# A two-layer hybrid decoder step: the order of every engine's instructions planned with the timeline model in place of the plain one

## The chip, the cores and the metric

The kernel runs on one core of one Trainium2 chip, in one launch. The metric is the device time of that launch in microseconds; smaller is better. Three timed runs of the kernel before gave 1852.14, 1854.70 and 1857.76 us (median 1854.7).

The core has five engines with an instruction stream each: TensorE (PE in the profile, with its weight loads apart as PEld), VectorE (DVE), ScalarE (ACT), GpSimd (POOL) and SyncE (SP, which here issues nearly all DMAs). Each engine runs its own stream in order, and an instruction that waits for another engine or for a DMA holds up what stands behind it on its engine. So the order of each stream is part of the program.

## The reference, cut to what matters

Two groups of tokens share all weights: a prompt of 256 tokens that starts from zero state, and 8 sequences of 4 new tokens that bring their states along. That is 288 columns, which are carried through together. Two layers follow one another:

```
x = x + 0.5 * swiglu(rmsnorm(x), w_ffn1_gu, w_ffn1_down)          # 1024 -> 2 x 2816 -> 1024
u = rmsnorm(x);  q,k,v,g,a,z,xbc,dt,gate_a,gate_b = split(u @ w_in)
log_a  = log_sigmoid(a @ w_gla_a2 + b) / 16
o_gla  = rmsnorm(gla_chunked(q, k, v, log_a, state_gla)) * silu(g)  # gated linear attention, 4 heads
xs,B,C = split(silu(causal_conv(xbc, state_conv)))
y      = ssd_chunked(xs, softplus(dt + dt_bias), -exp(a_log), B, C, state_ssm) + d_skip * xs
y      = rmsnorm(y * silu(z))                                       # state space part, 32 heads
m      = sigmoid(gate_a) * (o_gla @ w_proj_gla) + sigmoid(gate_b) * (y @ w_proj_ssm)
x = x + m @ w_out
x = x + 0.5 * swiglu(rmsnorm(x), w_ffn2_gu, w_ffn2_down)
...
return rmsnorm(x), new_gla, new_ssm, new_conv                       # states of both groups
```

All inputs and outputs are float32.

## The kernel before, in words

**Big products.** The activations lie transposed, 128 channels by 288 tokens. A float32 product is made of three products in a reduced type (float32r): `weights` (L171) loads a block of 1024 x 128 weights (512 KB) by SP into `wr` (4 buffers), `split` makes its high part `wh` on ScalarE (L158) and the rest `wl = wr - wh` on VectorE (L164; 3 buffers each), and `mm3` runs 24 matmuls of 128 x 128 by 128 x 288 on it: eight pairs `wh` x high and low activations (L177, L178) and eight `wl` x high (L180), all into one PSUM tile `psg` (3 buffers, in places 7).

**Stages of a layer.** `ffn` is 44 such blocks for gate and up, then 24 for the way down; VectorE and ScalarE have a few instructions of 288 columns beside each. `mixer` has `gla` first (the projections q, k, v, then the attention in small matmuls of full float32 into `pst` tiles, 4 buffers) and then `ssd`, which goes through 16 pairs of heads, j = 0 to 15. For each j there is a chain over the engines: `stage_x` (conv: ACT L851, DVE L852, L853, ACT L856, three times DVE L858, ACT L860, DVE L862), `stage_m` (transposes on PE L142, `m` on ACT L1010 to L1014, `xg` on DVE L1018, `xd` on POOL L1021) and `stage_y` (PE L1044 to L1051, DVE L1053, POOL L1059, ACT L1061, DVE L1063; state update PE L1069, DVE L1071). `stage_bc` and `stage_group` (PE L926 to L928, DVE L923) come once for 4 of the j.

**Fillers.** `gla` and `ssd` are generators. At each `yield n` the loop `run` traces n steps of `fillers`, which are the big products that depend on neither: z (16 blocks), g (8), then gate and projection of the GLA branch, then the last gate. So in the traced program small chains alternate with blocks of `mm3`.

**What sets the order.** The program is traced once, in the order of the Python code, inside `tile.TileContext(nc)`. When the context closes, a list scheduler plays the traced program on a model of the machine. When an engine of the model is free, it takes of that engine's instructions those whose inputs are there (in the model) and whose buffers are free, and of those the one traced first. What it takes is the engine's instruction stream; buffers and semaphores follow from it. On the chip the stream is fixed: an instruction that the model thought ready, and that is not, is waited for. In the program as built, 604 of TensorE's 13,077 matmuls stand ahead of one that was traced earlier, 964 of VectorE's 2,202 instructions, and 270 of SP's 809 DMAs. There are no priorities or due times written by hand besides the order of the code.

The lines that the change touches are the opening of the context in `kernel`:

## Time and profile before

| | |
|---|---|
| median of three runs | 1854.7 us |
| the profiled execution | 1855.64 us, of it 1853.4 us span from the first to the last instruction |
| TensorE busy | 1816.3 us (98%), 13,712 matmuls |
| weight loads of TensorE (PEld) | 1750.2 us (94%) |
| VectorE / ScalarE / GpSimd busy | 1292.0 (70%) / 1035.5 (56%) / 237.1 us (13%) |
| mean granted TensorE clock | 0.993 |
| moved by DMA | 325 MB, 176 GB/s in the mean |

Busy time is the time in which at least one instruction of the engine runs. Matmuls are pipelined: a block of equal matmuls shows some 300 ns for each record, while they start 133 ns apart. The idle time before an instruction is put down to the one that ended last of those it waited for. The granted clock is 1.00 where TensorE runs at its full 2.4 GHz; a lower mean says for what share of a stretch it was at 1.2 GHz.

### The profile page before, as it was taken

The numbers are of one execution on the slowest core, as the hardware profiler recorded it, in microseconds if no ns is written. First come the engines' busy times: TensorE is split into PE (matmuls) and PEld (weight loads), VectorE is DVE, ScalarE is ACT, GpSimd is POOL, SyncE is SP. The second block draws the span as 40 slices with busy tenths as digits, with TensorE's granted clock in tenths as the row PEclk, the third lists the DMA queues.
The fourth block names the chain that finished last, engine by engine and source line by source line (L and its number), as shares of the span: only waits on it lengthen the run. The fifth ranks groups of instructions, "written<-read, shape, count | busy, mean of one in ns | idle before, by whom it ended". The sixth has DMA issues, their size and how long they took to land. (4 is left out here: it accounts for less than half of the span.)

```text
span 1853.4 us, 34776 instructions
## 1 busy us (share of the span) xinstructions
PE 1816.3 (98%) x13712; PEld 1750.2 (94%) x13712; DVE 1292.0 (70%) x2202; ACT 1035.5 (56%) x1818; POOL 237.1 (13%) x305
## 2 busy tenths in 40 slices
PE   8999999999999999999999999999999999999998
PEld 8999999888899899999999999998889998999997
DVE  6555577689989767555565556776999887665554
ACT  6444466566767646444454445665776675454443
POOL 1000000024435300000000000000444443000000
PEclk9999999999999999999999999999999999999999
DMA  7555654866777655555555556568667775655553
GB/s 210 165 168 158 167 140 128 265 184 177 211 213 208 179 167 170 170 166 164 166 168 163 165 158 166 136 184 246 166 186 219 199 217 156 176 160 169 160 161 93
DMA packets 613111, 325.41 MB, mean 176 GB/s; under 512 B 17090, under 2 KB 607986, under 8 KB 612948
## 3 DMA queue, kind: packets, MB, share of 16 engines
q1 hardware_dynamic: 612900, 323.07, 61.7%
q8 instruction: 107, 1.75, 0.4%
q14 instruction: 56, 0.46, 0.1%
q10 hardware_dynamic: 48, 0.13, 0.0%
HBM read 292.93 MB, written 30.22 MB: 174 GB/s over the span
## 5 line engine op out<-in xcount | busy, mean ns | idle before, releaser
L158 ACT ACTIVATE wh<-wr 128x1024 fp32r<-128x1024 f32 (+1 forms) x498 | 518.0, 1041 | 470.6 <-PE psg L178 384.9
L177 PE MATMUL psg<-xh,wh 128*128 128x288 f32 x2704 | 744.0, 301 | 3.0 <-DVE cbuf L853 2.3
L178 PE MATMUL psg<-xl,wh 128*128 128x288 f32 x2704 | 738.1, 299 | 0.1
L164 DVE TENSOR_TENSOR wl<-wr,wh 128x1024 fp32r<-128x1024 f32 (+1 forms) x496 | 602.8, 1215 | 147.9 <-ACT wh L158 147.1
L177 PEld LDWEIGHTS psg<-xh,wh 128*128 128x128 f32 x2704 | 511.4, 190 | 9.9 <-issue 6.3
L178 PEld LDWEIGHTS psg<-xl,wh 128*128 128x128 f32 x2704 | 511.5, 189 | 3.5 <-issue 0.9
L180 PE MATMUL psg<-xh,wl 128*128 128x288 f32 x2704 | 416.2, 296 | 0.0
L180 PEld LDWEIGHTS psg<-xh,wl 128*128 128x128 f32 x2704 | 378.6, 189 | 1.1 <-issue 0.9
L177 PE MATMUL psg<-hh,wh 128*128 128x288 f32 x704 | 189.7, 296 | 0.0
L178 PE MATMUL psg<-hl,wh 128*128 128x288 f32 x704 | 189.4, 295 | 0.0
L304 DVE TENSOR_TENSOR t<-t,psg 128x288 f32<-128x288 f32 x88 | 40.0, 454 | 135.2 <-ACT wh L158 123.1
L178 PEld LDWEIGHTS psg<-hl,wh 128*128 128x128 f32 x704 | 132.8, 189 | 0.0
L177 PEld LDWEIGHTS psg<-hh,wh 128*128 128x128 f32 x704 | 132.4, 188 | 0.1
L180 PE MATMUL psg<-hh,wl 128*128 128x288 f32 x704 | 109.2, 296 | 0.0
L301 DVE TENSOR_TENSOR t<-psg,rr 128x288 f32<-128x288 f32 x88 | 40.2, 457 | 90.4 <-PE psg L180 90.4
L180 PEld LDWEIGHTS psg<-hh,wl 128*128 128x128 f32 x704 | 98.9, 188 | 0.0
L858 DVE SCALAR_TENSOR_TENSOR cacc<-cbuf,cw,cacc 128x312 f32<-128x312 f32 x144 | 86.6, 601 | 9.5 <-ACT cacc L856 8.9
L1037 POOL TENSOR_TENSOR st<-st,decs 128x512 f32<-128x512 f32 x64 | 83.5, 1323 | 25.5 <-PE pst L142 24.2
L371 POOL MEMSET cbuf<- 128x3 f32 x4 | 0.3, 108 | 654.6 <-DVE t L324 654.6
L177 PE MATMUL psg<-yh,wh 128*128 128x288 f32 x256 | 70.0, 300 | 0.0
L178 PE MATMUL psg<-yb,wh 128*128 128x288 f32 x256 | 69.2, 297 | 0.8 <-DVE yb L1063 0.8
L177 PE MATMUL psg<-oh,wh 128*128 128x288 f32 x256 | 69.7, 300 | 0.0
(312 smaller groups left out, 2322.9 us busy)
## 6 DMA issues: line engine op xcount, KB each, us to landing
wr<-in_w_ffn_gu_dram SPq DMA_DIRECT2D x176, 512.0 KB
wr<-in_w_in_dram SPq DMA_DIRECT2D x160, 512.0 KB
wr<-in_w_ffn_down_dram SPq DMA_DIRECT2D x64, 448.0 KB
wr<-in_w_ffn_down_dram SPq DMA_DIRECT2D x32, 512.0 KB
st<-in_state_ssm_dram SPq DMA_DIRECT2D x64, 256.0 KB
out_dram<-st SPq DMA_DIRECT2D x64, 256.0 KB
wr<-in_w_proj_ssm_dram SPq DMA_DIRECT2D x32, 512.0 KB
gst<-in_state_gla_dram SPq DMA_DIRECT2D x32, 256.0 KB
```

The source lines that it names most:

```text
L158: A.activation(out=h, in_=raw, func=AF.Copy)
L164: V.tensor_tensor(out=lo, in0=raw, in1=h, op=ALU.subtract)
L177: T.matmul(out, lhsT=h[:, k], rhs=xh[k], start=start and k == 0, stop=False)
L178: T.matmul(out, lhsT=h[:, k], rhs=xl[k], start=False, stop=False)
L180: T.matmul(out, lhsT=lo[:, k], rhs=xh[k], start=False, stop=stop and k == n - 1)
L301: V.tensor_tensor(out=t, in0=pg, in1=r, op=ALU.mult)
L304: V.tensor_tensor(out=h, in0=t, in1=pu, op=ALU.mult)
L371: G.memset(cbufs[i][:, 0:3], 0.0)
L858: V.scalar_tensor_tensor(out=acc, in0=buf[:, i:i + NCV], scalar=w[i], in1=acc, op0=ALU.mult, op1=ALU.add)
L1037: G.tensor_tensor(out=sts[hf], in0=sts[hf], in1=bcast(decs[:, 8 * j + hf:8 * j + 8:2], 2, 128), op=ALU.mult)
```

## The change

`TileContext` gets one more argument. The scheduler then plays the same traced program on another model of the machine, one that follows each instruction through the parts it occupies (the engine's queue, its start, the tail of its write, the clock and the passes of the TensorE array, the DMA queues); the plain model is coarser. Nothing else is edited: the same instructions are traced, with the same shapes, operands and buffers, and the same number of DMAs. What may differ is the order in each of the five streams, and with it which of a tag's buffers a tile gets, where a semaphore is waited for, and where ScalarE has to change its function tables.

```diff
@@ -1246,7 +1246,7 @@
     for i, shape in enumerate(_OUTS):
         args.append(nc.dram_tensor(f"out_{i}_dram", shape, F32, kind="ExternalOutput").ap())
-    with tile.TileContext(nc) as tc:
+    with tile.TileContext(nc, schedule_with_timeline_sim=True) as tc:
         tile_hybrid_step(tc, *args)
     r = run_bass_kernel_spmd(nc, [arrays], core_ids=[0])
```

## Rows read from the trace of the kernel before

**Rows 1.** The page, part 1: busy time, share and instructions of each engine.
```profile
span 1853.4 us, 34776 instructions
PE 1816.3 (98%) x13712; PEld 1750.2 (94%) x13712; DVE 1292.0 (70%) x2202; ACT 1035.5 (56%) x1818; POOL 237.1 (13%) x305
```

**Rows 2.** Windows by stage: first FFN, mixer, two FFNs, mixer, last FFN.
```profile
0.00:236.26 236.26, 230.98 (x1683) 227.10 (x1684) 136.79 (x198) 116.19 (x164) 7.46 (x15) 1.00 0.61 172
236.26:697.86 461.60, 449.55 (x3431) 419.69 (x3430) 378.04 (x718) 294.17 (x598) 113.84 (x143) 0.99 0.68 188
697.86:1149.96 452.10, 451.98 (x3402) 450.57 (x3401) 263.74 (x372) 217.84 (x297) 1.05 (x5) 1.00 0.57 165
1149.96:1608.58 458.62, 448.02 (x3431) 417.97 (x3430) 376.85 (x719) 293.61 (x598) 114.62 (x141) 0.99 0.68 189
1608.58:1853.40 244.82, 235.76 (x1773) 234.85 (x1771) 136.59 (x199) 113.68 (x165) 0.11 (x1) 0.99 0.51 149
```

**Rows 3.** Windows of 50 us: length, busy PE PEld DVE ACT POOL, clock, DMA.
```profile
100.00:150.00 50.00, 50.00 (x376) 50.00 (x375) 27.51 (x39) 23.23 (x32) 0.00 (x0) 1.00 0.55 159
250.00:300.00 50.00, 48.53 (x348) 46.09 (x348) 36.22 (x83) 29.95 (x59) 0.00 (x0) 0.97 0.46 123
350.00:400.00 50.00, 47.49 (x337) 42.33 (x336) 33.36 (x62) 29.97 (x59) 5.84 (x13) 0.97 0.73 207
400.00:450.00 50.00, 46.06 (x349) 42.72 (x348) 49.03 (x94) 32.48 (x70) 22.19 (x27) 0.93 0.60 165
1300.00:1350.00 50.00, 44.56 (x329) 41.52 (x330) 46.87 (x97) 36.66 (x84) 21.47 (x30) 0.95 0.54 148
1350.00:1400.00 50.00, 47.88 (x370) 44.65 (x369) 48.33 (x87) 33.09 (x71) 20.43 (x26) 0.98 0.78 215
```

**Rows 4.** Waits of PE, whole run: total us, times, longest.
```profile
PE psg L142 <- DMA xi<-in_x_prompt_dram: 4.7, 1, 4.7
```

**Rows 5.** Waits of PE in the first mixer (236 to 698 us).
```profile
PE pst L1044 <- DVE xg L1018: 2.3, 2, 1.8
PE pst L142 <- DVE t L138: 0.8, 1, 0.8
```

**Rows 6.** Waits of PE in the second mixer (1150 to 1608.6 us).
```profile
PE pst L142 <- DVE b L138: 1.5, 1, 1.5
```

**Rows 7.** Timeline of PE, 429 to 438 us: start, length, idle before.
```profile
429.97 0.31 PE L928 MATMUL pst<-bcf,b 128*128 128x32 f32 x2
432.07 0.66 PE L1044 MATMUL pst<-m,xg 128*64 128x256 f32 x4 [1.79 <-DVE xg L1018]
...
435.21 0.80 PE L1069 MATMUL pst<-bm,xpk 128*128 128x512 f32 x1 [1.39 <-ACT sh L967]
...
437.37 0.44 PE L177 MATMUL psg<-xh,wh 128*128 128x288 f32 x1
437.61 0.44 PE L178 MATMUL psg<-xl,wh 128*128 128x288 f32 x1
```

**Rows 8.** Timeline of ACT in the same stretch, the last split ahead of it.
```profile
428.83 1.04 ACT L158 ACTIVATE wh<-wr 128x1024 fp32r<-128x1024 f32 x1
```

**Rows 9.** Timeline of DVE, 263 to 265 us.
```profile
263.59 1.20 DVE L164 TENSOR_TENSOR wl<-wr,wh 128x1024 fp32r<-128x1024 f32 x1
264.72 0.21 DVE L138 COPY t<-t 128x128 f32<-128x128 f32 x1
```

**Rows 10.** Groups of PE and DVE by line: count, busy us, mean ns, idle before.
```profile
L1069 PE MATMUL pst<-bm,xpk 128*128 128x512 f32 x64 | 25.3, 461 | 4.6 <-ACT sh L967 2.8 <-DVE bpk L923 1.7
L1018 DVE TENSOR_TENSOR xg<-pst,dtt 128x384 f32<-128x384 f32 x32 | 17.5, 547 | 0.0
```

**Rows 11.** Groups of ACT by line: one of the lines with table loads.
```profile
L607 ACT ACT_TABLE_LOAD x6 | 7.7, 1283 | 0.1
```

**Rows 12.** Waits of SP's queue: total us, times, longest.
```profile
SPq L171 <- DVE wl L164: 740.3, 268, 12.7
SPq L1073 <- DVE st L1071: 38.8, 42, 2.2
```

## The prediction, made before the result was known

> **What bounds the kernel now.** I read the page's busy shares first, then windows by stage, then windows of 50 us, and last the waits and timelines where a window showed a hole. The shares say TensorE: 1816.3 us busy of a span of 1853.4 [rows 1]; 1853.4 - 1816.3 = 37.1 us is all that it idles. The windows by stage put a place to it [rows 2]: 236.26 - 230.98 = 5.3 us in the first FFN, 461.60 - 449.55 = 12.05 us in the first mixer, 0.1 us in the 452 us of the two FFNs between, 458.62 - 448.02 = 10.6 us in the second mixer, and 244.82 - 235.76 = 9.1 us in the last FFN. The first of these is nearly all one wait of 4.7 us for the first input [rows 4], and the last lies behind the last block: output and its transfer. Neither depends on which ready instruction an engine takes first. In the FFN a window of 50 us holds 376 matmuls without a hole, 133 ns each, with VectorE at 27.5 and ScalarE at 23.2 of 50 [rows 3]: no order can speed that up, and there is slack enough that few would slow it.
>
> So the change can act in the mixers, 920 us. There it can gain the idle 12.05 + 10.6 = 22.65 us, and with it what the clock costs: five windows show a granted mean under 1 [rows 3], short by 0.03, 0.03, 0.07, 0.05 and 0.02 of 50 us, together 10.0 us of full-speed work. Where the clock fell, TensorE had just been waiting: after holes of 1.79 and 1.39 us the matmuls start 0.24 us apart, 437.37 to 437.61 [rows 7], which is the 1.2 GHz level, against 0.133 before. I cost a clock loss that goes away with its holes at the whole 10.0 at most. The ceiling of a gain is then 22.65 + 10.0 = 32.65 us.
>
> **The change part by part.** It removes and adds no instruction; it permutes five streams. I take them in turn.
>
> *TensorE's stream.* What can go is a wait of its head while something behind it is ready. The trace shows that such work was there. At 430.28 (429.97 + 0.31) TensorE stops for 1.79 us before L1044, whose `xg` was late on VectorE; later for 1.39 us before L1069; and the first block behind them, at 437.37, needs a `wh` [rows 7]. The last split that ScalarE made ahead of it ended at 428.83 + 1.04 = 429.87 us [rows 8], before the hole began. So 16 matmuls on that `wh`, 16 x 0.133 = 2.1 us, could have stood in front of L1044 and filled its hole; the plain model evidently thought `xg` ready sooner than it was. Both mixers lose most of their idle in holes of this kind [rows 5, 6]: 1 to 2 us for a VectorE or ScalarE result of the chain, with a block behind. Bounds: a model that gets the durations right recovers between nothing (it moves the holes) and all 22.65 us. I take half, 11.3: rows 7 show one hole that a block covers and, 3 us on, a second for which only the rest of that block would be left.
>
> *What the new order brings of its own.* The two mixers are the same code on the same shapes, planned in different circumstances, and they wait at different places: the largest wait of the first is 1.8 us for `xg` [rows 5], of the second 1.5 us for the packed `b` [rows 6]. They take 461.60 and 458.62 us [rows 2]. So 3.0 us per mixer is what an order of this kind is worth by chance, and I charge the new one 2 x 3.0 = 6.0 us of new waits. The clock follows the holes: half of 10.0, so 5.0 comes back.
>
> *VectorE's stream.* At 400 to 450 us it is busy 49.03 of 50 us [rows 3]; its 378 us of work in a mixer of 461.6 [rows 2] don't bound the whole, but there its order decides what TensorE gets. A split `wl` (L164) of 1.20 us was put ahead of the copy L138 of 0.21 us at 263.59 [rows 9], and TensorE waited 0.8 us for the copy [rows 5]. An order could undo such picks or make more of them; this price is in the rival below, and in the forecast inside the two terms above.
>
> *ScalarE's stream.* It is 56% busy [rows 1], so its moves are hidden under TensorE except in the chains. One thing could be added: a function table load costs 1.283 us [rows 11], and another order of `Exp` and `Ln` in the decay chain could add or save some. L607 has 6 of them; 6 more would be 7.7 us on ScalarE and, since it idles 167 of 461.6 us of a mixer [rows 2], I cost them at nothing; uncovered, at 7.7.
>
> *SP's and GpSimd's.* SP's queue waits for its buffers, not the other way round: the weight loads L171 wait 740 us for `wl` to free a raw tile [rows 12]. A state store L1073 put ahead of a load holds it up by at most 2.2 us [rows 12]; a load runs up to four blocks of 24 x 0.133 = 3.2 us ahead, which hides it. Without that cover each of the 42 such waits would cost up to 2.2 us, and that I leave to the range. GpSimd is 13% busy [rows 1]: nothing, unless its one multiply in the chain is picked late, for which the same cover serves.
>
> **The sum.** The profiled execution took 1855.64 us, 2.2 more than its span. 1855.6 - 11.3 + 6.0 - 5.0 = 1845.3. That execution lies 0.9 us over the median of the runs, so a median of 1844 to 1846; I say 1845. Its own range: three quarters of the ceiling, 1855.6 - 0.75 x 32.65 = 1831, to a gain that can just be told, 1849.
>
> [...]
>
> **The rivals.**
>
> 1. *Slower: splits ahead of the chain.* One mechanism: the new model fills the short gap between two dependent VectorE instructions with the next ready `wl` split, as in [rows 9], at each of the 32 steps j. TensorE's price was 0.8 us there, 1.8 us at worst [rows 5]. There are 32 steps, by the count of L1018 [rows 10]: 32 x 0.8 = 25.6 us, and 32 x 1.8 = 57.6 at the far end. It decides from 10.3 / 0.8 = 13 such steps on, where it has eaten the gain. Time: 1855.6 + 25.6 = 1881. For it: VectorE is at 94 to 98% where `ssd` begins [rows 3], so what is put off there comes late. Against it: most of the 32 steps run without a wait now, under a model that could err the same way.
>
> 2. *No change.* Where an engine's head is ready it is taken under either model, and the streams are alike; the few holes move. Time 1855.6 +- 3. For it: even in the emptiest of those windows TensorE is busy 44.56 of 50 us [rows 3]. With it goes that the change does not do what it says, and the streams come out the same: 1855.
>
> 3. *Faster than the idle allows.* The mixers' weight loads are busy 419.69 and 417.97 us, 29.9 and 30.05 us less than the matmuls [rows 2]. If an order closed half of these 60 us as well: 1845 - 30 = 1815. Against it: the difference has a cause that no order removes, wide matmuls such as L1069, whose 512 columns take 461 ns a record [rows 10] beside a block's 300.
>
> **How the numbers follow.** Forecast 0.44, slower 0.31, no change 0.19 and the same streams 0.04, the third rival 0.02. With a bound of 0.3%, 5.6 us, which is what a measurement of this kernel can tell from nothing, faster is under 1849 and slower over 1860. Faster: 0.44 + 0.02 = 0.46. Same: 0.19 + 0.04 = 0.23. Slower: 0.31. The range goes down to 1830, just under the forecast's own, which leaves out the third rival and a recovery of nearly all (some 0.05), and up to 1885, over rival 1 at 0.8 us a step, which leaves out its far end (some 0.12). The forecast's own range is 1831 to 1849.
>
> **What would show it.** Right: PE busy sum unchanged near 1816, the two mixers 452 to 457 us each, idle in them near 9 us each, the windows at the start of `ssd` with a clock nearer to 1; the FFN windows still 376 matmuls without a hole; in the timeline, blocks of L177 and L178 in front of L1044 and L1069 where these wait now. Rival 1: new PE waits on `xg`, `b` or `yos` at many j, with a L164 just ahead on VectorE. Rival 2: mixers within 3 us of now. The prediction would be wrong in its foundation if an FFN stage changed, if TensorE's busy time fell, or if the order of SP's DMAs made weights late, with PE waiting for `wh` or `wl`.

## The result, and the profile after

The kernel after took 1877.6 us (median of 4 runs, 1877.1 to 1878.2), the kernel before 1855.1 us beside it. The ratio is 1.0123, 95% interval 1.0111 to 1.0135: slower by 22 us, where 1845 us was forecast. The profiled execution took 1877.1 us with a span of 1875.3, 21.9 us over the span of [rows 1]. Part 1 of its page:

```profile
span 1875.3 us, 34869 instructions
PE 1826.6 (97%) x13712; PEld 1753.4 (93%) x13712; DVE 1309.7 (70%) x2202; ACT 1030.9 (55%) x1818; POOL 250.4 (13%) x305
```

The 21.9 us are two things: TensorE idles 48.7 us instead of 37.1 (+11.6), and the same 13,712 records keep it busy for 1826.6 us instead of 1816.3 (+10.3).

Next the windows by stage, cut at two points found in both traces, VectorE's last L324 of an FFN and its last L540 of a mixer. First mixer, FFNs between, second mixer; columns as in [rows 3]. Before:

```profile
226.85:718.68 491.83, 479.77 (x3656) 449.35 (x3655) 402.21 (x754) 315.40 (x630) 114.89 (x148) 0.99 0.68 187
718.68:1140.55 421.87, 421.75 (x3177) 420.92 (x3176) 239.56 (x335) 196.62 (x265) 0.00 (x0) 1.00 0.57 165
1140.55:1629.40 488.85, 478.25 (x3656) 447.63 (x3655) 400.20 (x753) 313.56 (x628) 115.67 (x146) 0.99 0.67 187
```

After:

```profile
226.81:729.52 502.71, 485.12 (x3656) 450.54 (x3655) 409.31 (x753) 312.89 (x630) 123.32 (x148) 0.99 0.65 183
729.52:1150.95 421.43, 421.31 (x3177) 420.67 (x3176) 239.34 (x336) 196.77 (x265) 0.00 (x0) 1.00 0.57 165
1150.95:1650.84 499.89, 483.68 (x3656) 449.82 (x3655) 408.48 (x753) 311.53 (x628) 120.31 (x146) 0.99 0.65 183
```

The FFNs are as they were. Each mixer is longer by 10.9 and 11.0 us, and in each TensorE idles more: 502.71 - 485.12 = 17.6 us against 12.1, and 16.2 against 10.6. The two are now wrong in the same way, so this is no chance hole.

The waits of TensorE in the whole run name new heads (total, times, longest):

```profile
PE psg L177 <- DVE dal L584: 7.5, 2, 3.8
PE psg L177 <- DVE ob L475: 5.2, 2, 2.6
...
PE yo L978 <- DVE yos L983: 3.8, 1, 3.8
...
PE yo L978 <- ACT sh L967: 2.2, 1, 2.2
```

The waits of [rows 5, 6] for `xg` and the packed `b` are gone from this list. In their place stand, first of all, waits for a PSUM buffer: the first block of a `psg` can't start before VectorE has read the one that had the buffer (`dal`, `ob`), nor the next `yo` before `yos` has. TensorE's stream is rearranged far more than it was: in the order of before 604 of its 13,077 matmuls stand ahead of one traced earlier, in that of after 2082.

The largest is at the start of each mixer. TensorE before, then after (start, length, idle before):

```profile
230.00 0.32 PE L178 MATMUL psg<-xl,wh 128*48 128x288 f32 x1
230.16 1.21 PE L180 MATMUL psg<-xh,wl 128*48 128x288 f32 x8
231.21 0.65 PE L268 MATMUL pst<-nacc,call 128*128 128x288 f32 x2
```

```profile
232.65 0.29 PE L178 MATMUL psg<-xl,wh 128*48 128x288 f32 x1
232.78 1.20 PE L180 MATMUL psg<-xh,wl 128*48 128x288 f32 x8
233.82 0.65 PE L268 MATMUL pst<-nacc,call 128*128 128x288 f32 x2
240.59 0.58 PE L177 MATMUL psg<-xh,wh 128*128 128x288 f32 x1 [3.76 <-DVE dal L584]
```

VectorE, before and after:

```profile
233.32 1.95 DVE L281 RECIPROCAL rr<-rr 128x288 f32<-128x288 f32 x1 [0.59 <-ACT rr L280]
235.19 1.16 DVE L164 TENSOR_TENSOR wl<-wr,wh 128x1024 fp32r<-128x1024 f32 x1
236.26 0.43 DVE L584 TENSOR_TENSOR dal<-psg,rr 48x288 f32<-48x288 f32 x1
```

```profile
229.38 0.52 DVE L253 SCALAR_TENSOR_TENSOR xl<-xt,prm,xh 128x288 fp32r<-128x288 f32 x1 [0.61 <-ACT xh L252]
...
235.93 1.95 DVE L281 RECIPROCAL rr<-rr 128x288 f32<-128x288 f32 x1 [0.59 <-ACT rr L280]
237.80 2.29 DVE L164 TENSOR_TENSOR wl<-wr,wh 128x1024 fp32r<-128x1024 f32 x2
240.01 0.44 DVE L584 TENSOR_TENSOR dal<-psg,rr 48x288 f32<-48x288 f32 x1
```

The last `xl` is written at 229.90 (229.93 before). Before, TensorE takes it at 230.00; after, it first does nearly all `wh` matmuls of two q blocks and takes it at 232.65. So the sum of squares (L268) is 2.61 us later, the reciprocal as much, and with two splits instead of one ahead of it (2.29 us for 1.16) `dal` is 3.75 us later: 2.61 us of that come from TensorE's order, the rest from VectorE's. The three `psg` buffers hold `pd` and two q blocks, and `pd` is free only when `dal` is made. Before, TensorE has other matmuls in hand until then; after, it has done them already and stands for 3.76 us. The window of 10 us with this hole and the one behind it, where the granted clock falls to 0.70 in the mean (length, busy PE PEld DVE ACT POOL, clock, DMA):

```profile
230.00:240.00 10.00, 6.84 (x50) 6.42 (x48) 5.56 (x5) 4.73 (x5) 0.90 (x3) 0.96 0.34 97
240.00:250.00 10.00, 9.41 (x51) 9.35 (x52) 8.02 (x16) 6.20 (x9) 0.00 (x0) 0.70 0.45 122
```

Before, the same two windows hold 76 matmuls each at 1.00:

```profile
230.00:240.00 10.00, 10.00 (x76) 9.78 (x75) 8.05 (x12) 6.44 (x8) 0.90 (x3) 1.00 0.54 152
240.00:250.00 10.00, 10.00 (x76) 9.84 (x75) 7.92 (x13) 9.85 (x13) 0.00 (x0) 1.00 0.59 160
```

The second kind of place is in `ssd`. VectorE after, ahead of the wait for `yos`:

```profile
484.79 1.21 DVE L164 TENSOR_TENSOR wl<-wr,wh 128x1024 fp32r<-128x1024 f32 x1
485.93 0.53 DVE L858 SCALAR_TENSOR_TENSOR cacc<-cbuf,cw,cacc 128x312 f32<-128x312 f32 x1
486.38 1.05 DVE L1063 SCALAR_TENSOR_TENSOR yb<-yb,prm,yh 128x288 fp32r<-128x288 f32 x1
487.35 0.53 DVE L858 SCALAR_TENSOR_TENSOR cacc<-cbuf,cw,cacc 128x312 f32<-128x312 f32 x1
487.81 1.21 DVE L164 TENSOR_TENSOR wl<-wr,wh 128x1024 fp32r<-128x1024 f32 x1
488.94 0.41 DVE L983 TENSOR_TENSOR yos<-yo,eAs 128x256 f32<-128x256 f32 x1
```

and TensorE and the windows:

```profile
489.50 1.07 PE L978 MATMUL yo<-sh,cz 128*32 128x256 f32 x4 [3.81 <-DVE yos L983]
```

```profile
480.00:490.00 10.00, 5.92 (x52) 4.37 (x50) 10.00 (x16) 6.05 (x14) 5.08 (x4) 0.92 0.74 205
490.00:500.00 10.00, 7.99 (x47) 7.06 (x44) 6.89 (x21) 4.60 (x11) 2.20 (x6) 0.74 0.24 62
```

VectorE is busy 10.00 of 10 us while TensorE stands, with two splits in the queue ahead of the small operation that frees `yo`. That looks like rival 1, and was tried below.

### The profile page after: what moved, and what is told of

The parts are those of the page before. It is cut to its first block, busy times and chain, and to the rows that moved or that the text cites. A ratio compares the mean times of both kernels' runs of the same rounds, so it can differ in the third digit from the quotient of the medians.

```text
span 1875.3 us, 34869 instructions
## 1 busy us (share of the span) xinstructions
PE 1826.6 (97%) x13712; PEld 1753.4 (93%) x13712; DVE 1309.7 (70%) x2202; ACT 1030.9 (55%) x1818; POOL 250.4 (13%) x305
## 4 chain that ended last, share of the span: by engine, by line
PE 55%; DVE 4%; ACT 0%; DMA 0%; issue 0%; SPq 0%; DVEq 0%; ACTq 0%
PE psg L177 17%; PE psg L178 17%; PE psg L180 16%; PE pst L142 1%; DVE wl L164 1%; DVE cacc L858 1%; PE pst L1044 0%; PE yo L978 0%; PE pst L1069 0%; DMA acb<-acd 0%; PE pst L787 0%; PE gyo L778 0%; ACT wh L158 0%; SPq L955 0%; PE pst L1047 0%
## 5 line engine op out<-in xcount | busy, mean ns | idle before, releaser
L164 DVE TENSOR_TENSOR wl<-wr,wh 128x1024 fp32r<-128x1024 f32 (+1 forms) x496 | 608.9, 1228 | 150.3 <-ACT wh L158 145.7
L858 DVE SCALAR_TENSOR_TENSOR cacc<-cbuf,cw,cacc 128x312 f32<-128x312 f32 x144 | 82.7, 574 | 9.7 <-ACT cacc L856 8.1
L178 PE MATMUL psg<-ob,wh 128*128 128x288 f32 x256 | 69.3, 296 | 0.0
```

The source lines that it names most:

```text
L164: V.tensor_tensor(out=lo, in0=raw, in1=h, op=ALU.subtract)
L178: T.matmul(out, lhsT=h[:, k], rhs=xl[k], start=False, stop=False)
L858: V.scalar_tensor_tensor(out=acc, in0=buf[:, i:i + NCV], scalar=w[i], in1=acc, op0=ALU.mult, op1=ALU.add)
```

## The experiments

All are timed against the kernel before on the same chip (its median lay between 1852.7 and 1855.2 us).

**The mixer's start, taken back.** `start` is the kernel after with two limits on the order: L268 holds back TensorE's matmuls of the second and later q blocks, L584 VectorE's splits of the third and later ones (the lines that name the two instructions are not shown).

```diff
+            qb = blocks([W[:, O_Q:O_Q + 1024]], norm.x, 8)
+            for j in range(8):
+                with ExitStack() as behind:
+                    if j >= 1:
+                        behind.enter_context(tc.issue_after(norm.sum.ins))   # L268
+                    if j >= 2:
+                        behind.enter_context(tc.issue_after(scaled.ins))     # dal, L584
+                    _, (pg,) = next(qb)
```

> The kernel after (1877.1 us), with the start of each mixer in another order: TensorE may start the second and later q blocks only behind the matmul that sums the squares (L268), VectorE the splits of the third and later blocks only behind dal (L584). Theory A (two separate holes per mixer, one at its start behind dal and one at the start of ssd; the trace of after has 6.4 and 5.3 us of excess over the usual spacing of matmuls in 240 to 250 and 1160 to 1170): both starts come back, the waits for dal of 3.8 us go, 1877 - 11.7 = 1865, between 1862 and 1869. Theory B (the mixer as a whole is paced by VectorE's work in ssd, and time won at the start is waited for there): waits for dal go, the time stays within 4 us of 1877. Theory C (VectorE slower beside GpSimd's operations, 18.7 us more busy time): no change, 1875 to 1879, as no operation of GpSimd is touched.

1866.7 us, ratio 1.0057 (1.0042 to 1.0072): 10.9 us under the kernel after. Theory A said 1865. The wait for `dal` shrank to

```profile
PE psg L177 <- DVE dal L584: 1.9, 2, 1.0
```

Theories B and C fall for this half: time won there is kept, with GpSimd's operations as they were (VectorE's extra busy time, 18.7 us in the expectation, is 17.7). The gain is made where the hole was. TensorE and VectorE of `start`, and the two windows of above:

```profile
232.53 0.65 PE L268 MATMUL pst<-nacc,call 128*128 128x288 f32 x2
```

```profile
236.70 0.45 DVE L584 TENSOR_TENSOR dal<-psg,rr 48x288 f32<-48x288 f32 x1
```

```profile
230.00:240.00 10.00, 9.04 (x67) 8.65 (x66) 5.26 (x6) 6.10 (x8) 0.90 (x3) 1.00 0.13 37
240.00:250.00 10.00, 10.00 (x75) 9.84 (x74) 9.64 (x15) 8.16 (x11) 0.00 (x0) 1.00 0.96 261
```

These are 142 matmuls for the 101 of after; at 133 ns each the 41 are 5.5 us, the whole gain of one mixer. ScalarE also has four table loads fewer in `start` (28 for 32), but the first that goes stands at 252.06 us in after, behind these windows. `start` lifts both delays at once: L268 comes 1.29 us earlier than in after, and no split stands ahead of `dal`, which comes 3.31 us earlier. It can't tell what each is worth.

`before_late` puts TensorE's part alone into the kernel before: an edge that holds L268 behind the second q block's `wh` matmuls.

```diff
+                if j == 1:
+                    tc.add_manual_dep(norm.sum.ins, mark[0].ins.name, ... NoSync ...)
```

> The kernel before (1855.1 us), with one edge: the matmul that sums the squares (L268) may be issued only behind the second q block's matmuls with wh (all but the last), so some 14 matmuls or 1.9 us later, as the timeline order has it; all else is left as it was. Theory A (this place alone costs half of the loss): a wait for dal of 2 to 3 us at each mixer's start and a lower clock behind it, 3.5 to 6 us a mixer, 1862 to 1867. Theory B (time lost here is made up in the mixer): 1853 to 1858.

1859.4 us, 1.0021 (1.0010 to 1.0032). The waits came as expected:

```profile
PE psg L178 <- DVE dal L587: 5.6, 2, 2.8
```

but they cost 4.2 us in all, not 7 to 12: the time lies between the ranges of theories A and B. A window 20 us on, first of before and then of this kernel, shows where some of it came back:

```profile
260.00:270.00 10.00, 8.86 (x55) 8.23 (x55) 7.37 (x17) 2.54 (x5) 0.00 (x0) 0.83 0.90 244
```

```profile
260.00:270.00 10.00, 10.00 (x78) 9.73 (x77) 9.96 (x20) 4.74 (x6) 0.00 (x0) 1.00 0.59 162
```

The kernel before has a hole of its own there, and with the earlier hole this one is gone. A hole costs what it adds to the ones that it replaces.

**One engine's stream at a time.** For each engine, a helper adds edges between neighbours of a given order, so that this stream is fixed instruction for instruction, while the model orders the other four:

```diff
+        for a, b in zip(order, order[1:]):
+            tc.add_manual_dep(ins[b], ins[a].name, ... NoSync ...)
```

> The timeline model makes the order of all engines, but TensorE's stream is held to that of the kernel before, instruction for instruction. Theory P (the loss is in TensorE's stream: it has 2082 of 13,077 matmuls ahead of an earlier-traced one instead of 604, so short steps of the chain come late and its head waits for a PSUM buffer): back to before, 1853 to 1860. Theory V (the loss is in VectorE's stream, splits L164 ahead of operations of the chain): VectorE's order is still the model's own, so 1867 to 1877. Theory A: the hole at the mixer's start is one of TensorE's order, that at the start of ssd one of VectorE's: 1862 to 1869.

> The plain model makes the order, but TensorE's stream is held to that of the kernel after, instruction for instruction. Theory P: 1870 to 1880. Theory V: 1853 to 1862. Theory A: the wait for dal at the mixers' start is there (some 6 us each), that of ssd is not: 1862 to 1869.

> The plain model makes the order, but VectorE's stream is held to that of the kernel after, instruction for instruction. Theory P: 1853 to 1862. Theory V: 1870 to 1880. Theory A: 1860 to 1868, with no wait for dal over 2 us at the mixers' start.

1882.5 us (1.0143), 1877.0 us (1.0115), 1917.7 us (1.0339). The first fits none of P, V and A, the third is worse than any theory allowed. The second fits theory P alone, but by its time only: its longest wait, 10.9 us in all for `qk` L664, is in neither kernel. With one stream fixed the other four get a third order, neither that of before nor that of after, and lose time of their own: `tl_pe_before` waits 3.7 us for `xl` L351, where before doesn't wait for it and after 0.6 us. These three settle nothing on whose stream is to blame; in them one stream taken from either order beside four others lost time against before. ScalarE's, GpSimd's and SP's streams were not tried.

**Splits held back on VectorE.** Rival 1's mechanism, on top of `start` and on the kernel before:

```diff
+            with ExitStack() as behind:
+                if len(freed) >= 2:
+                    behind.enter_context(tc.issue_after(freed[-2]))
                 V.tensor_tensor(out=lo, in0=raw, in1=h, op=ALU.subtract)
```

(`freed` gathers L467, L475, L852 and L983; `behind3` has 3 for 2.)

> The kernel start (1866.7 us), and on VectorE a split (L164) may be issued only behind the last but one operation that frees a PSUM buffer (of z, g, the convolution's blocks and yo) traced before it. Theory A with splits (what is left of the loss is at the start of ssd, where VectorE does splits ahead of the operation that frees a buffer for which TensorE's head waits: ob 5.2, cbuf 3.9, yos 2.6, yb 1.8 us in start): half of these 13.5 us and the clock lost behind them go, 1856 to 1861. Theory D (in the first 90 us of ssd VectorE itself is the bound, 9.9 of 10 us busy, and an order of it only moves the wait): 1864 to 1869. Theory E (splits held back make TensorE wait for wl): over 1870, with waits for wl.

> As behind2, but a split stands behind the last but two such operations, so that fewer are held back. Theory A with splits: between start and behind2, 1858 to 1864. Theory D: 1864 to 1869. Theory E: between 1867 and behind2.

> The kernel before (1855.1 us) with the rule of behind2 and the plain model. Theory A with splits: it waits only 2.3 us for freed buffers (cbuf), so a gain of at most 3 us, 1851 to 1856. Theory D: 1853 to 1857. Theory E: over 1858, with waits for wl.

1877.6 us (1.0120), 1869.7 us (1.0074) and 1877.1 us (1.0110). Theory A with splits falls. E's ranges hold in all three (in `behind3` 0.7 us over D's), but the wait for weights that E names comes only in the kernel before,

```profile
PE psg L184 <- DVE wl L168: 19.6, 16, 2.7
```

while on top of `start` (`behind2`) no wait for `wl` is seen, and the waits move to the convolution:

```profile
PE pst L937 <- DVE bcf L873: 9.5, 2, 5.3
PE psg L181 <- DVE ob L479: 5.5, 4, 1.6
```

A split seen ahead of a late operation is not yet the cause of its lateness: in the kernel before, the block behind that split is what TensorE lives on.

**One part of the mixer at a time.** Here the helper fixes all five streams, but only among the instructions traced in one part (`held`); the model orders the rest.

```diff
+        order = [n for n in order if ins[n].name in held]
```

> The timeline model makes the order, but among the instructions traced in gla (the first part of a mixer, with the fillers traced between), those of all five engines keep the relative order of the kernel before; the ssd part and the FFNs are the model's. Theory A (two separate losses that add: 10.4 us of the 22 at the mixers' starts, as the kernel start showed, the rest in the ssd part): 1864 to 1869. Theory G (all of it comes from the gla part, the ssd part only hands it on): 1853 to 1859. Theory S (the loss is in the ssd part and start won time there by luck of another order): 1872 to 1880.

> The other half: what is traced from ssd's first instruction to the end of the mixer keeps the order of the kernel before, gla is the timeline model's. Theory A: 1877.1 - 11.6 = 1865.5, 1863 to 1869. Theory G: 1873 to 1880. Theory S: 1853 to 1859.

> The plain model makes the order, but what is traced in gla keeps the relative order of the kernel after on all five engines. Theory A: 1855.1 + 10.4 = 1865.5, 1862 to 1869. Theory G: 1873 to 1880. Theory S: 1853 to 1859.

> The plain model makes the order, but what is traced from ssd's first instruction to the end of the mixer keeps the relative order of the kernel after. Theory A: 1855.1 + 11.6 = 1866.7, 1863 to 1870. Theory G: 1853 to 1859. Theory S: 1873 to 1880.

1870.7, 1869.1, 1860.1 and 1872.9 us (1.0084, 1.0076, 1.0027, 1.0099). Both parts lose, so G and S fall. A's ranges are missed too, by 0.1 to 2.9 us on either side: the two losses don't simply add. After's order of `gla` costs 5.3 us in the kernel before, and taking it out of the kernel after brings 6.9. After's order of `ssd` costs 18.1 us, and taking it out brings 8.5. What a part is worth hangs on the order of the other.

**What in `ssd`.** A `yo` is 16 records of L978; before, they run as 16 whole groups, after, as 31 pieces, and the busy time of the line (count | busy us, mean ns) went from

```profile
L978 PE MATMUL yo<-sh,cz 128*32 128x256 f32 x256 | 17.1, 385 | 0.0
```

to

```profile
L978 PE MATMUL yo<-sh,cz 128*32 128x256 f32 x256 | 25.1, 392 | 6.0 <-DVE yos L983 3.8 <-ACT sh L967 2.2
```

Those 8.0 us are most of the 10.3 that TensorE was busy longer. So the groups were made whole again, with and without the limits of `start` (the changed loops are below), and halved in the kernel before (that edit is not shown):

```diff
-                for h in range(2):
-                    for r in range(4):
+                with tc.high_priority():
+                    for h in (1, 0):
+                        for r in (3, 2, 1, 0):
 ...
```

> The kernel start (1866.7 us), with the groups of yo (L978) whole: their matmuls come in the reverse order, so that the first needs the last sh, and at a high priority, so that no other matmul lies between. Candidate H (a group costs 1.0 us whole; in start its pieces of 2, 4, 8 and 12 records take 0.55, 0.56, 0.57 and 0.99 us and 0.23 us to enter, some 3.7 us a mixer more, and the 2.6 us wait for yos and a part of the 5.2 us for ob hang on them): 1866.7 - 7 to 12 = 1855 to 1860. Candidate J: the waits go to other heads, 1864 to 1869.

> The kernel after (1877.1 us), with the groups of yo whole as in whole, and its mixers' starts as they are. Candidate H: 1866 to 1871. Candidate J: 1874 to 1880.

> The kernel before (1855.1 us, plain model), with each group of yo traced in two halves of 8 records, the first as soon as two of the four sh are there. Candidate H: 2 x (0.57 + 0.23) - (1.0 + 0.22) = 0.38 us a group, 6 us for 16, and what waits for the one PSUM buffer, 1860 to 1866. Candidate J (pieces as such cost nothing): 1853 to 1857.

1865.1 us (1.0062, 1.0048 to 1.0075), 1876.0 us (1.0119) and 1854.1 us (1.0004, 0.9995 to 1.0013). H falls, J holds. In `whole` the line is back at 17.1 us and TensorE's busy time at 1817.5, and the waits are longer instead:

```profile
PE pst L142 <- DVE bcf L869: 8.7, 2, 5.3
PE psg L177 <- DVE ob L475: 7.2, 2, 3.6
```

(0.6 and 5.2 us in `start`). Then stretches of `ssd` were fixed to before's order in the kernel after: iterations 2 to 6, and what lies ahead of them, by `held` again.

> The kernel after (1877.1 us), with what is traced in ssd's iterations j = 2 to 6, of 16, held to the relative order of the kernel before; all else is the timeline model's. Theory M (the ssd part's loss arises in these iterations, where VectorE is busy 10 of 10 us and TensorE's stream has done some 40 filler matmuls fewer than before's at the sixth step): nearly what ssd_before brought, 1869 to 1872. Rival N (the order before these steps, in gla and ssd's first iterations, sets it): 1874 to 1880.

> The kernel after (1877.1 us), with what is traced from ssd's first instruction to its iteration j = 1 held to the relative order of the kernel before; iterations 2 to 15, the projection, gla and the FFNs are the timeline model's. Rival N (the order of ssd's first steps sets the loss of the part): 1867 to 1872, as ssd_before. Joint (no stretch of ssd has it; an order is good only as a whole, and the model's continuation behind a held stretch loses the time again): 1873 to 1880.

1875.6 us (1.0110) and 1878.2 us (1.0132). Neither stretch brings the time that the whole part brings. What the timeline order loses in `ssd` was found neither in the splits nor in the `yo` groups nor in one of these two stretches (iterations 7 to 15 were not tried by themselves); it stays open which picks make it.

**A kernel faster by 0.2%.** `gla_start` is the kernel before with `held` all of `gla`, in the order of `start`.

> The kernel before (plain model), with what is traced in gla held to the relative order of the kernel start instead of after (gla_after with after's order took 1860.1 us; its two waits for dal took 3.8 us each and some 6 us a mixer with the clock). Theory A (the start of the mixer is a hole of its own, and the rest of gla's timeline order is no worse than before's): 1860.1 - 10.4 = 1849.7, 1847 to 1853, below before (1855). Rival K (what gla wins, ssd waits for, as VectorE is the bound there): 1853 to 1858.

1851.2 us (10 runs), ratio 0.9981 (0.9972 to 0.9990). Theory A said 1849.7; rival K falls. Without its hole at the start, the timeline model's order of `gla` is better than the plain one by 3.8 us: 1860.1 - 1851.2 = 8.9 us is what the hole costs there, a price like that of `start`. `gla_start` also makes 28 table loads on ScalarE where before and `gla_after` make 32, as in `start`; no run shows what share of the 3.8 and the 8.9 us is theirs.

## Why the prediction was wrong

*What bounds the kernel.* Right: TensorE, and only the mixers moved; an FFN stage changed by 0.4 us of 422, and SP's order made no weights late. The sign that I had named for a wrong foundation did not come.

*TensorE's stream, -11.3.* This step failed. The holes that I named did close: `xg`, `bpk` and `b` are gone from TensorE's waits, and L1069 no longer waits. But I bounded the step below by nothing, "it moves the holes", and took a ready block in front of a waiting matmul for a pure gain. Such a block is taken from later. At the mixer's start the new order filled a gap with two q blocks; 7 us on, TensorE had nothing left but a block without a buffer, and the chain, which could have gone on at 229.90, was 3.75 us late. The step's true lower end is a loss. That is shown for the mixers' starts, 10.9 of the 22 us (`start`). The rest lies in the order of `ssd`, where the runs give its size and no cause. (In the working, the split that ended at 429.87 is the last ahead of the hole, not of the block at 437.37; another ran from 432.20 to 433.24. A `wh` was ready all the same: the split made from 424.98 to 426.02 was still unused.)

*New waits, +6.0.* Right in sign, mis-sized. I took the spread of two mixers under one model, 3.0 us, for what another order could cost. They share the model and so its errors: both new mixers lost 11 us, each with the same hole at its start. TensorE's idle grew by 5.5 and 5.6 us in them, and the time that its matmuls keep it busy by 5.4 each.

*The clock, -5.0.* Nothing came back: the mean over the span went from 0.993 to 0.992. The holes changed place, and the clock fell behind the new ones (0.70 and 0.74 in the windows above).

*"PE busy sum unchanged."* Wrong by 10.3 us. The Trainium skill says on the page "Perfetto Trace Analysis", section "Identifying the Most-Contended Engine", that matmul busy time is not a good measure of how close a kernel is to the roofline, and that the share of the peak rate and the busy share of weight loading are to be used instead. The trace agrees that busy time misleads: for the same matmuls busy time grew by 10.3 us, weight loading by 3.2, and `whole` is busy 7.7 us less than `start` for 1.6 us less time.

*Rival 1, 1881 us.* The time was near by luck. Its sign, waits on `xg`, `b` or `yos` at many j, did not come: there is one of 3.8 us on `yos`. One more split does stand in front of `dal` and makes 1.14 of its 3.75 us, and `start` took both away with the rest; held back as a rule, splits cost more than they save (`behind2`, `before_behind2`). At the start TensorE's own order made the larger part of the delay, and without the added split it gave waits of 2.8 us (`before_late`).

*SP, GpSimd, ScalarE at nothing.* ScalarE's busy time fell by 4.6 us with 32 table loads as before, and SP's loads caused no new wait; no run here moved one of these alone.

## What to carry to other kernels

A list order that keeps the bottleneck engine busy now spends the work that would cover a later latency; before counting a filled hole as a gain, look at what is left in front of the next wait, and which buffer the filler takes with it. A new order of all engines is judged whole: here single streams and single stretches taken from the order of before did not bring back its time, and only a whole part (`gla`) with its one visible hole mended did better than both kernels. The spread between two repeats under one plan says nothing of another plan's price.

## What the runs showed of the hardware that was not expected

The same 2202 VectorE instructions took 17.7 us longer, and GpSimd's same 305 took 13.3 us longer, by their order alone. Two rows of after, the same 24-column copy beside GpSimd's work and alone:

```profile
480.36 1.02 DVE L853 COPY cbuf<-scf 128x24 f32<-128x24 f32 x1
...
494.74 0.19 DVE L853 COPY cbuf<-scf 128x24 f32<-128x24 f32 x1
```

Over the trace, L853 takes 181 ns on average (at most 190) in the 38 cases in which no GpSimd instruction runs at that time, and 713 ns (up to 1071) in the 10 with one. Of these 10, GpSimd's instruction started first in 8, and the copy ended 42 to 47 ns after that instruction's end; in the other two the copy started first and took 170 and 171 ns. The Trainium skill says on the page "SBUF — State Buffer", section "SBUF: two separate sides", that GpSimd and a VectorE instruction in a two-port mode or with two SBUF inputs hold a shared pair of ports by an exclusive lock, whichever starts first keeping it for its whole length; the trace agrees for this copy, though no run shows in which mode it is. That this stretching cost time here is not shown: with GpSimd busy 250.6 us, as in after, `start` won its 10.9 us all the same.

A group of 16 `yo` records, 128x32 weights and 256 columns, took 1.00 us from its start to that of the next matmul when it ran whole; a piece of 8 took 0.57 us, and one of 4 took 0.56, more than twice its share. In the kernel's time this could not be seen: with nearly all groups halved, `before_halves` took as long as before.
